# A decoder block's modulation rows: products moved into the mLSTM's chunk loop, four accumulators, other engines for some transfers

## The chip, the cores and the metric

The kernel runs on one core of one Trainium2 chip. The metric is the device time of one execution in microseconds (us). A core has TensorE (PE, with its weight loads shown apart as PEld), VectorE (DVE), ScalarE (ACT), GpSimd (POOL) and SyncE (SP). Any of SP, ACT and POOL can issue a transfer; each engine takes its instructions strictly in the order in which they stand in its program, and a transfer that must wait holds up what stands behind it on the engine that issues it.

## The reference

One decoder layer over 1024 tokens of width 1024. Six rows of 1024 numbers, the modulation, are a product of one vector with a 1024 x 6144 matrix; the rows gate1, shift2, scale2 and gate2 (numbers 2 to 5) are the ones that the change is about. One of the four mixers is an mLSTM that carries a state from one chunk of 128 tokens to the next.

```python
cond = jax.nn.silu(c)
mod = cond @ w_ada[layer] + b_ada[layer]
shift1, scale1, gate1, shift2, scale2, gate2 = jnp.split(mod[:, None, :], 6, axis=-1)
h = rms_norm(x, w_norm1) * (1.0 + scale1) + shift1
x = x + gate1 * hybrid_mixer(h, w_in, w_out, ...)
h = rms_norm(x, w_norm2) * (1.0 + scale2) + shift2
x = x + gate2 * hierarchical_moe(h, ...)
...
def mlstm_chunkwise(q, k, v, i_pre, f_pre):   # one chunk of 128 tokens at a time
    ...
    C_new = scale * C + einsum('blhd,blhe->bhde', vc * w_s, kc)
    w = einsum('bcthd,bcshd->bctsh', q, k) * exp(log_d - m_t)
    num = einsum('bctsh,bcshd->bcthd', w, v) + inter * einsum('bchde,bcthe->bcthd', C_in, q)
```

## The kernel before

A first stage (about 0 to 80 us) norms the input, makes the rows shift1 and scale1, and leaves the normed input transposed in SBUF as a high and a low half, `hH` and `hL`. Then come the projections with `w_in`, block of 256 columns by block: `load_w` brings a block in two halves of 512 KB (four of the eight row tiles each) into the buffer `wraw`, of which there is one; ACT copies a half to its high part `wh`, and DVE subtracts to get the low part `wl` (function `split`, L53 and L61). Each projection is three products per row tile, (wh, hH), (wl, hH) and (wh, hL), in one PSUM tile of the pool `ps` (two buffers) that ACT evicts. The mLSTM's four blocks are LQ and LK (products of 128x512), then LV and LO (128x256, eight groups of 24 each); the sigmoid of LO's groups, `so`, goes to DRAM (`so_d`) and is read back later as `ym`.

Beside these, `modulation` makes the four rows. For each row, DVE accumulates eight tiles of `w_ada` times a column of `cond` into the tile `macc` (L552 the first, L554 the others); the tiles `mw`, 512 KB each in three buffers, are loaded by SP (L550). Then TensorE sums over the partitions with two products of a column of ones and a half of `macc` (written `pq<-macc,ones`), DVE adds the bias row (L562, for the third row L564 too), and ACT stores the row to `mod_d`. There is one `macc`.

Behind the projections of the mLSTM stands its loop over eight chunks t. A chunk takes a broadcast row block `rb` (SP), the products `pq<-qT,kT`, the exponentials `ex` on DVE and ACT, DVE's products of `ex` with those scores (L612), the products `pq<-va,ex`, and from the second chunk on `pq<-C,qT` with the state; a transpose of `kT`, products `pq<-vw,kt` and four DVE steps (L647) make the next state. Between the chunks' products TensorE takes the projections of the next block group, MX0 to MX2 (`ssd_inputs`): their `wraw`, `wh` and `wl` are made in the meantime, their groups are evicted by ACT as `craw` and `xbc`, and three DVE steps (L680) and a SiLU make the convolution.

A scheduler sets the order of the instructions on each engine over this whole stretch: it interleaves the projections, the modulation, the chunk loop and the MX blocks by its own estimates, so that code that stands behind in the text can stand ahead in an engine's program. What an engine's program holds is fixed once the kernel is built.

## Time and profile before

| | before |
|---|---|
| median of 3 runs | 1274.83 us (1273.33 to 1276.05) |
| profiled execution, its own time | 1273.05 us |
| its span | 1271.3 us |
| TensorE busy in it | 1153.3 us (91%) |
| DVE / ACT / POOL busy | 801.5 / 589.3 / 326.3 us |
| mean granted TensorE clock | 0.966 of full speed |

The span is what the trace covers, and the execution's own time is 1.75 us more. Times in the rows further down count from the span's start. A row of a timeline gives the start, the duration, the engine with the line of the code, the operation, what it writes and reads, how many instructions the row holds, and in brackets the idle time before it with what ended that idle time.

### The profile page before, as it was taken

The page shows a single profiled execution, that of the slowest core. Times are in us where ns is not written, and L with a number is a line of the kernel's source. Part 1 is how long each engine was busy: PE and PEld are TensorE (multiplying, and loading weights), DVE is VectorE, ACT ScalarE, POOL GpSimd, SP SyncE. Part 2 cuts the span into 40 slices and gives each one's busy share as a digit, 9 for nine tenths or more (in the row PEclk, how much of TensorE's full clock was granted, in tenths as well). Part 3 has the DMA queues.
Part 4 walks back from the last instruction along what each step waited for, and adds up shares of the span by engine and source line. Part 5 has one row for each costly group of instructions (what it writes and reads, how often), then busy time and mean ns, then how long its engine had stood idle before and what let it go on. Part 6 is the DMA issues. An engine that isn't in the chain of part 4 may idle for free. (4 is left out here: it accounts for less than half of the span.)

```text
span 1271.3 us, 18583 instructions
## 1 busy us (share of the span) xinstructions
PE 1153.3 (91%) x6455; PEld 868.1 (68%) x6455; DVE 801.5 (63%) x1460; ACT 589.3 (46%) x909; POOL 326.3 (26%) x314
## 2 busy tenths in 40 slices
PE   4689879999999899999959999999999999999981
PEld 3577667879998788787747754466676557665660
DVE  6976667757643488488878941335654564555674
ACT  6442114354743488344437841224553443554563
POOL 2420000002102277333321942102322132222111
PEclk8699999999999999999969999999999999999996
DMA  9614884222221123675477999999999998999975
GB/s 268 203 32 149 261 271 118 89 71 53 73 60 34 42 65 111 203 267 199 162 296 290 328 332 377 376 403 372 385 378 378 357 389 317 341 367 384 337 274 198
DMA packets 96452, 305.48 MB, mean 240 GB/s; under 512 B 15106, under 2 KB 53756, under 8 KB 71772
## 3 DMA queue, kind: packets, MB, share of 16 engines
q1 hardware_dynamic: 84762, 284.47, 60.9%
q0 software_dynamic: 8464, 17.13, 5.8%
q10 hardware_dynamic: 3122, 2.56, 0.6%
q8 instruction: 57, 0.93, 0.3%
q14 instruction: 47, 0.39, 0.1%
HBM read 283.86 MB, written 32.06 MB: 249 GB/s over the span
## 5 line engine op out<-in xcount | busy, mean ns | idle before, releaser
L1649 POOL DMA_INDIRECT x_d<-yt,tabi x34 | 62.1, 1827 | 240.7 <-DVE yt L1623 186.7
L56 PE MATMUL ps<-wu,xTs 128*64 128x512 f32 x256 | 119.5, 599 | 1.8 <-DMA wu<-in_w_expert_up_dram 1.8
L56 PE MATMUL ps<-wg,xTs 128*64 128x512 f32 x256 | 119.8, 599 | 0.0
L56 PE MATMUL ps<-wh,hH 128*128 128x256 f32 (+1 forms) x336 | 96.9, 289 | 8.2 <-ACT so L53 4.9
L56 PE MATMUL ps<-wl,hH 128*128 128x256 f32 (+1 forms) x336 | 95.8, 286 | 0.0
L56 PE MATMUL ps<-wh,hL 128*128 128x256 f32 (+1 forms) x336 | 95.2, 288 | 0.0
L56 PE MATMUL ps<-hH,wh 128*128 128x512 f32 x224 | 89.1, 398 | 0.5 <-ACT xbc L53 0.4
L56 PE MATMUL ps<-hH,wl 128*128 128x512 f32 x224 | 89.4, 399 | 0.0
L56 PE MATMUL ps<-hL,wh 128*128 128x512 f32 x224 | 89.0, 397 | 0.0
L56 PEld LDWEIGHTS ps<-wh,hH 128*128 128x128 f32 x336 | 64.4, 192 | 11.4 <-ACT so L53 5.5
L56 PE MATMUL ps<-split,xTH 128*128 128x512 f32 x200 | 69.4, 403 | 1.0
L56 PEld LDWEIGHTS ps<-wg,xTs 128*64 128x64 f32 x256 | 32.1, 136 | 54.6 <-issue 51.3
L1640 POOL TENSOR_TENSOR yt<-yt,g2bc 128x1024 f32<-128x1024 f32 x14 | 33.7, 2409 | 137.5 <-ACT yt L53 121.4
L53 ACT ACT_TABLE_LOAD x47 | 60.3, 1283 | 17.7 <-DVE xbc L680 5.9
L53 ACT ACTIVATE xTH<-pq 128x512 fp32r<-128x512 f32 x33 | 18.4, 592 | 100.9 <-PE pq L1664 100.9
L56 PE MATMUL ps<-wh,xTH 128*128 128x512 f32 (+1 forms) x156 | 63.8, 409 | 1.4 <-PEq L1869 0.5
L56 PEld LDWEIGHTS ps<-wl,hH 128*128 128x128 f32 x336 | 64.1, 191 | 0.9 <-issue 0.9
L61 DVE TENSOR_TENSOR wl<-wu,wh 128x1024 fp32r<-128x1024 f32 x39 | 47.2, 1222 | 27.4 <-ACT wh L53 26.7
L56 PEld LDWEIGHTS ps<-wh,hL 128*128 128x128 f32 x336 | 64.3, 194 | 0.0
L56 PE MATMUL ps<-wl,xTH 128*128 128x512 f32 (+1 forms) x156 | 61.3, 393 | 0.5 <-DVE wl L61 0.5
L56 PE MATMUL pq<-wd,aTs 128*64 128x512 f32 x256 | 58.7, 597 | 3.0 <-PEq L1857 2.1
L53 ACT ACTIVATE sg<-ps 128x512 f32<-128x512 f32 (+1 forms) x32 | 18.9, 592 | 91.1 <-PE ps L56 49.8
(550 smaller groups left out, 3241.2 us busy)
## 6 DMA issues: line engine op xcount, KB each, us to landing
wg<-in_w_expert_gate_dram SPq DMA_DIRECT2D x64, 1024.0 KB, 9.5
wu<-in_w_expert_up_dram SPq DMA_DIRECT2D x64, 1024.0 KB, 8.1
wd<-in_w_expert_down_dram SPq DMA_DIRECT2D x64, 1024.0 KB, 7.5
mw<-in_w_ada_dram SPq DMA_DIRECT2D x32, 512.0 KB, 5.0
wraw<-in_w_in_dram SPq DMA_DIRECT2D x20, 512.0 KB, 3.6
xt<-in_x_dram SPq DMA_DIRECT2D x16, 512.0 KB, 4.1
wt<-in_w_ada_dram SPq DMA_DIRECT2D x16, 512.0 KB, 5.4
woraw<-in_w_out_dram SPq DMA_DIRECT2D x16, 256.0 KB, 3.4
```

Of the source, the lines that this page charges most:

```text
L53: return nc.scalar.activation(o, i, f, **kw)
L56: return nc.tensor.matmul(o, l, r, start=start, stop=stop)
L61: (eng or nc.vector).tensor_sub(lo, src, hi.bitcast(F32))
L1640: nc.gpsimd.tensor_mul(yt[:, on_dve * 512:], yt[:, on_dve * 512:], g2bc[:, on_dve * 512:])
L1649: nc.gpsimd.indirect_dma_start(out=x1_d, out_offset=bass.IndirectOffsetOnAxis(ap=tok, axis=0), in_=yt, in_offset=None, bounds_check=S - 1, ...
```

## The change

`modulation` keeps four accumulators (`macc0` to `macc3`) and runs all 32 loads and accumulations on end. The eight products with ones, the additions of the bias rows and the stores move into a function `mod_rows` that the chunk loop calls ahead of its third chunk (t == 2). The bias rows now take buffers of the tag `mw` (as 1x1024 of a 128x1024 tile) and are loaded by SP; the rows are stored by POOL. `load_w` takes the engine that loads: LK, LV and LO are loaded by ACT, the other blocks still by SP. The stores of `so` go from SP to ACT. Behind the change the lines of the code stand lower by 10 (L612 is L622, L680 is L690).

```diff
@@ -123,7 +123,7 @@
     hH = hpool.tile([P, KT, S], F32R, name="hH")
     hL = hpool.tile([P, KT, S], F32R, name="hL")
 
-    def load_w(*ranges):
+    def load_w(*ranges, first=nc.sync):
         n = sum(b - a for a, b in ranges)
         wh = wp.tile([P, KT, 272], F32R, name="wh")
         wl = wp.tile([P, KT, 272], F32R, name="wl")
@@ -131,7 +131,7 @@
             raw = wp.tile([P, 4, 272], F32, name="wraw", bufs=1)
             o = 0
             for i, (a, b) in enumerate(ranges):
-                (nc.sync if i % 2 == 0 else nc.scalar).dma_start(
+                (first if i % 2 == 0 else nc.scalar).dma_start(
                     raw[:, :, o:o + b - a],
                     w_in[k0 * P:(k0 + 4) * P, a:b].rearrange("(k p) g -> p k g", p=P))
                 o += b - a
@@ -542,9 +542,10 @@
     tab_d = dram.tile([S * NE, 4], F32, name="tab_d")
 
     def modulation(mp):
-        for i in range(4):
+
+        accs = [mp.tile([P, D], F32, name=f"macc{i}", bufs=1) for i in range(4)]
+        for i, acc in enumerate(accs):
             cs = slice((2 + i) * D, (3 + i) * D)
-            acc = mp.tile([P, D], F32, name="macc", bufs=1)
             for k in range(KT):
                 wt = mp.tile([P, D], F32, name="mw", bufs=3)
                 nc.sync.dma_start(wt, w_ada[k * P:(k + 1) * P, cs])
@@ -552,20 +553,27 @@
                     nc.vector.tensor_scalar(acc, wt, cond[:, k:k + 1], None, op0=OP.mult)
                 else:
                     nc.vector.scalar_tensor_tensor(acc, wt, cond[:, k:k + 1], acc, op0=OP.mult, op1=OP.add)
-            mr = mp.tile([1, 2, D], F32, name="mr", bufs=1)
-            nc.scalar.dma_start(mr[:, 0, :], b_ada[:, cs])
-            if i == 2:
-                nc.scalar.dma_start(mr[:, 1, :], w_norm2)
-            for c in (slice(0, 512), slice(512, D)):
-                o = pq1()
-                mm(o[0:1], ones[:, 0:1], acc[:, c], True, True)
-                nc.vector.tensor_add(mr[:, 0, c], mr[:, 0, c], o[0:1])
-            if i == 2:
-                nc.vector.scalar_tensor_tensor(mr[:, 0], mr[:, 0], 1.0, mr[:, 1], op0=OP.add, op1=OP.mult)
-            nc.scalar.dma_start(mod_d[i:i + 1], mr[:, 0])
-
-
-    def mlstm(ml, wk):
+
+        def mod_rows():
+            for i in range(4):
+                cs = slice((2 + i) * D, (3 + i) * D)
+                mr = mp.tile([P, D], F32, name="mr", tag="mw", bufs=3)[0:1]
+                nc.sync.dma_start(mr, b_ada[:, cs])
+                if i == 2:
+                    wr2 = mp.tile([P, D], F32, name="wr2", tag="mw", bufs=3)[0:1]
+                    nc.sync.dma_start(wr2, w_norm2)
+                for c in (slice(0, 512), slice(512, D)):
+                    o = pq1()
+                    mm(o[0:1], ones[:, 0:1], accs[i][:, c], True, True)
+                    nc.vector.tensor_add(mr[:, c], mr[:, c], o[0:1])
+                if i == 2:
+                    nc.vector.scalar_tensor_tensor(mr, mr, 1.0, wr2, op0=OP.add, op1=OP.mult)
+                nc.gpsimd.dma_start(mod_d[i:i + 1], mr)
+
+        return mod_rows
+
+
+    def mlstm(ml, wk, mod_rows):
         qT = ml.tile([P, 2, S], F32, name="qT")
         kT = ml.tile([P, 2, S], F32, name="kT")
         va = ml.tile([P, NT, NH, VW], F32, name="va")
@@ -575,26 +583,28 @@
         for j in range(2):
             for th in range(2):
                 act(qT[:, j, th * 512:(th + 1) * 512], chan_major(w, j, th), AF.Copy)
-        w = load_w((LK, LK + GW))
+        w = load_w((LK, LK + GW), first=nc.scalar)
         for j in range(2):
             for th in range(2):
                 act(kT[:, j, th * 512:(th + 1) * 512], chan_major(w, j, th), AF.Copy, scale=0.125)
-        w = load_w((LV, LV + GW))
+        w = load_w((LV, LV + GW), first=nc.scalar)
         for t in range(NT):
             act(va[:, t, :, :DH], heads(tok_major(w, t)[:, :GW], GW), AF.Copy)
         num = ml.tile([P, NT, NH, VW], F32, name="num")
         so_d = dram.tile([S, GW], F32, name="so_d")
-        w = load_w((LO, LO + GW))
+        w = load_w((LO, LO + GW), first=nc.scalar)
         for t in range(NT):
             so = wk.tile([P, GW], F32, name="so", tag="ym")
             act(so, tok_major(w, t)[:, :GW], AF.Sigmoid)
-            nc.sync.dma_start(so_d[t * P:(t + 1) * P], so)
+            nc.scalar.dma_start(so_d[t * P:(t + 1) * P], so)
 
         C = [ml.tile([P, 2, 2 * VW], F32, name=f"C{i}") for i in range(2)]
         for i in range(2):
             nc.gpsimd.memset(C[i], 0.0)
         for t in range(NT):
             ts = slice(t * P, (t + 1) * P)
+            if t == 2:
+                mod_rows()
             rb = wk.tile([P, NH, P], F32, name="rb")
             nc.sync.dma_start(rb, bc_rows_2d(nrow_d[:, t, :]))
 
@@ -943,8 +953,7 @@
     ml = pool(m1, "ml", "right")
     mlw = pool(m1, "mlw", "right", 2)
     m2 = ExitStack()
-    modulation(pool(m2, "mp", "right"))
-    mlstm(ml, mlw)
+    mlstm(ml, mlw, modulation(pool(m2, "mp", "right")))
     m2.close()
     m3 = ExitStack()
     xbc = ssd_inputs(pool(m3, "sA", "left"))
```

How the engines' programs change is read from their orders. **SP ahead of the block MX0, before.** The rows run from the last accumulator's loads to the first read-back of `so`; `wraw` is the first half of MX0.

```order
L550 DMA mw<-in_w_ada_dram 128x1024 x3
L591 DMA so_d<-so 128x256
L550 DMA mw<-in_w_ada_dram 128x1024 x2
L591 DMA so_d<-so 128x256 x2
L134 DMA wraw<-in_w_in_dram 128x4x256
L591 DMA so_d<-so 128x256 x3
L658 DMA ym<-so_d 128x2x256
```

MX0's first half is issued between stores of `so`, whose waits it shares.

**SP at the same place, now.** These are the last 16 loads of `mw` and what follows them.

```order
L551 DMA mw<-in_w_ada_dram 128x1024 x16
L561 DMA mr<-in_b_ada_dram 1x1024 x3
L609 DMA rb<-nrow_d 128x4x128
L134 DMA wraw<-in_w_in_dram 128x4x256
L668 DMA ym<-so_d 128x2x256
```

The first half of MX0 stood between stores of `so`, with the chunk loop's `rb` of the fourth chunk already issued; now it stands behind all of `mw`, three bias rows and that `rb`. The third of the three `mr` takes a buffer of `mw` and must wait until the last accumulation has read it. LO's loads and the stores of `so` are gone from SP.

**DVE at the start of the chunk loop, before.** `ex<-ex,pq` are the products of the first chunk, `wl` is the low part of MX0's first half.

```order
L554 SCALAR_TENSOR_TENSOR macc<-mw,cond,macc 128x1024 x5
L562 TENSOR_TENSOR mr<-mr,pq_982 1x512
L562 TENSOR_TENSOR mr<-mr,pq_985 1x512
L671 MEMSET craw 128x3
L673 MEMSET xbc_2085 128x3 x2
L673 MEMSET xbc_2218 128x3 x2
L673 MEMSET xbc_2351 128x3 x2
L612 TENSOR_TENSOR ex<-ex,pq_1688 128x2x128
L612 TENSOR_TENSOR ex<-ex,pq_1689 128x2x128
L61 TENSOR_TENSOR wl<-wraw,wh 128x4x256
```

So the first chunk's two products came right behind the additions of the last row, and only then the low part.

**DVE at the same place, now.** `macc_854` is the fourth accumulator, `L617` makes the second chunk's `ex`.

```order
L555 SCALAR_TENSOR_TENSOR macc_854<-mw,cond,macc_854 128x1024 x7
L61 TENSOR_TENSOR wl<-wraw,wh 128x4x256
L622 TENSOR_TENSOR ex<-ex,pq_1650 128x2x128
L622 TENSOR_TENSOR ex<-ex,pq_1651 128x2x128
L617 SCALAR_TENSOR_TENSOR ex<-rb,u,mpos 128x128 x4
L622 TENSOR_TENSOR ex<-ex,pq_1689 128x2x128
L657 SCALAR_TENSOR_TENSOR C_1645<-C_1644,csp,pq_1672 64x65 x4
L622 TENSOR_TENSOR ex<-ex,pq_1690 128x2x128
L627 TENSOR_TENSOR num<-pq_1703,escol 128x260
```

The low part of MX0's first half stood behind the first chunk's two products and now stands ahead of them, directly behind the last accumulation; the additions of the bias row are gone from here.

**TensorE at the last of the four rows, before.** `ps_1627` is a group of LO.

```order
L56 MATMUL ps_1627<-wh,hL 128x256
L56 MATMUL ps_1627<-wh,hH 128x256
L56 MATMUL pq_982<-macc,ones 1x512
L56 MATMUL pq_985<-macc,ones 1x512
L56 MATMUL ps_1627<-wl,hH 128x256
```

The pair of products with ones stood in the middle of a group of LO.

**TensorE ahead of the third chunk, now.** `pq_1715` belongs to the second chunk's state, the last row to the third chunk's scores.

```order
L645 MATMUL pq_1715<-ident,kT 128x128 x2
L56 MATMUL pq_1732<-macc_851,ones 1x512
L56 MATMUL pq_1715<-vw,kt 64x65 x4
L56 MATMUL pq_1735<-macc_851,ones 1x512
L56 MATMUL pq_1741<-macc_852,ones 1x512
L56 MATMUL pq_1744<-macc_852,ones 1x512
L56 MATMUL pq_1752<-macc_853,ones 1x512
L56 MATMUL pq_1755<-macc_853,ones 1x512
L56 MATMUL pq_1762<-macc_854,ones 1x512
L56 MATMUL pq_1765<-macc_854,ones 1x512
L56 MATMUL pq_1771<-qT,kT 128x128
```

The products with ones came in pairs, each pair between products of a projection, ahead of the chunk loop; seven of the eight now stand on end between two chunks, with no projection between them.

**DVE behind the chunk loop, before.** `hnv`, `num` and `ym` belong to the mLSTM's norms, L680 is the first step of MX0's convolution.

```order
L653 TENSOR_TENSOR d_2056<-num 128x8
L519 SCALAR_TENSOR_TENSOR hnv<-hnv,d_2041 128x8
L654 SCALAR_TENSOR_TENSOR d_2056<-d_2056,escol 128x8
L528 RECIPROCAL hnv<-hnv 128x8 x2
L529 TENSOR_TENSOR num<-num,hnv 128x8x64 x2
L659 TENSOR_TENSOR ym<-ym,num 128x512 x2
L517 TENSOR_REDUCE hnv<-hnq 128x8
L680 SCALAR_TENSOR_TENSOR xbc_2085<-craw,cols,xbc_2085 128x1024
```

The convolution's first step followed on the norms' steps, with no `wl` among them.

**DVE at the same place, now.** The rows begin with the first half of MX1.

```order
L61 TENSOR_TENSOR wl<-wraw,wh 128x4x256
L683 MEMSET xbc_2219 128x3 x2
L683 MEMSET xbc_2352 128x3 x2
L528 RECIPROCAL hnv<-hnv 128x8 x2
L529 TENSOR_TENSOR num<-num,hnv 128x8x64 x2
L669 TENSOR_TENSOR ym<-ym,num 128x512 x2
L517 TENSOR_REDUCE hnv<-hnq 128x8
L690 SCALAR_TENSOR_TENSOR xbc_2086<-craw,cols,xbc_2086 128x1024
```

The two `wl` of the block MX1, which stood inside the chunk loop, now stand here: the first ahead of this piece, the second two rows behind it, ahead of the second step of the convolution.

## Rows read from the trace of the kernel before

**Rows 1.** The page, busy time: busy us (share of the span) xinstructions.

```profile
PE 1153.3 (91%) x6455; PEld 868.1 (68%) x6455; DVE 801.5 (63%) x1460; ACT 589.3 (46%) x909; POOL 326.3 (26%) x314
```

**Rows 2.** Windows: stretch, length, busy us per engine, granted clock, DMA share, GB/s.

```profile
120.00:140.00 20.00, 17.61 (x78) 12.30 (x77) 12.24 (x12) 2.86 (x4) 0.00 (x0) 0.91 0.81 262
140.00:160.00 20.00, 18.41 (x145) 16.65 (x144) 14.99 (x18) 3.51 (x7) 2.44 (x2) 1.00 0.88 274
160.00:180.00 20.00, 16.39 (x125) 14.43 (x125) 13.93 (x16) 4.57 (x8) 0.00 (x0) 1.00 0.78 264
180.00:200.00 20.00, 15.14 (x110) 12.71 (x111) 9.14 (x15) 2.82 (x6) 0.00 (x0) 1.00 0.56 189
200.00:220.00 20.00, 20.00 (x157) 15.86 (x158) 18.35 (x58) 12.43 (x21) 2.50 (x4) 1.00 0.47 127
```

**Rows 3.** Waits, 112 to 200 us: total us, times, longest us.

```profile
DVE macc L554 <- DMA mw<-in_w_ada_dram: 12.8, 13, 1.6
...
PE ps L56 <- ACT so L53: 4.9, 3, 3.0
PE pq L56 <- DVE macc L554: 4.5, 2, 2.9
```

**Rows 4.** Timeline of SP, 110 to 200 us: issues of loads.

```profile
112.06 20.15 SPq L550 DMA_DIRECT2D mw<-in_w_ada_dram  x11
...
172.26 1.14 SPq L599 DMA_DIRECT2D rb<-nrow_d  x1
173.46 0.64 SPq L134 DMA_DIRECT2D wraw<-in_w_in_dram  x1
```

**Rows 5.** Timeline of DVE, 108 to 215 us.

```profile
116.62 1.23 DVE L61 TENSOR_TENSOR wl<-wraw,wh 128x1024 fp32r<-128x1024 f32 x1 [4.37 <-ACT wh L53]
...
118.60 2.60 DVE L554 SCALAR_TENSOR_TENSOR macc<-mw,cond,macc 128x1024 f32<-128x1024 f32 x2
...
130.57 1.28 DVE L554 SCALAR_TENSOR_TENSOR macc<-mw,cond,macc 128x1024 f32<-128x1024 f32 x1 [1.25 <-DMA mw<-in_w_ada_dram]
133.55 0.68 DVE L562 TENSOR_TENSOR mr<-mr,pq 1x512 f32<-1x512 f32 x1 [1.70 <-PE pq L56]
...
191.20 1.28 DVE L554 SCALAR_TENSOR_TENSOR macc<-mw,cond,macc 128x1024 f32<-128x1024 f32 x1 [1.25 <-DMA mw<-in_w_ada_dram]
...
201.40 1.23 DVE L61 TENSOR_TENSOR wl<-wraw,wh 128x1024 fp32r<-128x1024 f32 x1
```

**Rows 6.** Timeline of ACT, 172 to 202 us.

```profile
181.15 1.06 ACT L53 ACTIVATE wh<-wraw 128x1024 fp32r<-128x1024 f32 x1 [5.47 <-DMA wraw<-in_w_in_dram]
```

**Rows 7.** Issues of transfers, whole run: count, KB each, median us to landing.

```profile
mw<-in_w_ada_dram SPq DMA_DIRECT2D x32, 512.0 KB, 5.0
wraw<-in_w_in_dram SPq DMA_DIRECT2D x20, 512.0 KB, 3.6
...
rb<-nrow_d SPq DMA_DIRECT2D x8, 256.0 KB, 6.3
```

**Rows 8.** Timeline of TensorE, 128 to 202 us.

```profile
131.96 3.27 PE L56 MATMUL pq<-macc,ones 128*1 128x512 f32 x4 [2.39 <-issue]
...
192.66 1.88 PE L56 MATMUL pq<-macc,ones 128*1 128x512 f32 x4
...
201.10 1.16 PE L56 MATMUL pq<-va,ex 128*128 128x130 f32 x8
```

**Rows 9.** Timeline of TensorE and window, 70 to 76 us.

```profile
71.58 1.09 PE L289 MATMUL pq<-ident,acc 128*128 128x128 f32 x4 [4.46 <-DVE acc L211]
...
72.00:74.00 2.00, 2.00 (x11) 2.00 (x10) 1.33 (x8) 0.17 (x1) 0.27 (x1) 0.50 0.00 0
```

**Rows 10.** Timelines of ACT and TensorE behind the chunk loop.

```profile
242.84 1.28 ACT L53 ACT_TABLE_LOAD   x1 [2.40 <-DVE xbc L680]
...
246.41 0.51 PE L56 MATMUL ps<-hH,wh 128*128 128x512 f32 x1 [0.39 <-ACT xbc L53]
```

**Rows 11.** Stores of POOL: issue to landing.

```profile
nrow_d<-nrow POOLq DMA_DIRECT2D x1, 16.0 KB, 1.7
```

## The prediction

> **What bounds the kernel now.** I read the page first. TensorE is busy for 91% of the span [rows 1], so the change can gain where TensorE waits, and lose where it gives TensorE something to wait for. The windows of 20 us over the stretch that the change touches show where that is [rows 2]: TensorE is busy for 17.61, 18.41, 16.39 and 15.14 of 20 us from 120 to 200, and for all 20 of them from 200 to 220, when the chunk loop runs between MX projections. So 12.45 us are idle from 120 to 200, and none in the loop. The list of waits [rows 3] says what ended these idle times. The accumulations wait 12.8 us for their tiles, 13 times, TensorE 4.5 us for the accumulations (the products with ones stand in its program ahead of projections that are ready), and 4.9 us for evictions of LO, which hang on stores of `so` that SP issues late among the loads. Transfers fill 0.78 to 0.88 of the DMA engines' time from 120 to 180 [rows 2]: the stretch is bound by the modulation's 16 MB, and TensorE waits wherever the two are tied together.
>
> **What is untied.** With the products gone from between the projections, and LO's loads and the `so` stores off SP, nothing holds the projections of LK, LV and LO but their own weights. The last product before the chunk loop's `va,ex` would be ready 12.45 us of waits and four pairs of products earlier. A pair is 1.88 us [rows 8], a row of four records, so one product takes 0.94; the first pair took 3.27. That is 12.45 + 3.27 + 3 x 1.88 = 21.4 us, so TensorE would stand at the chunk loop at about 201.1 - 21.4 = 180 in place of 201.1 [rows 8].
>
> **What it is tied to instead.** On DVE the first chunk's products `ex<-ex,pq` now stand behind the last accumulation and behind `wl` of MX0's first half, and on SP that half is issued behind the third bias row, which waits for the last accumulation's buffer. So the loop begins at the end of the accumulations plus a chain, however early TensorE is there.
>
> The end of the accumulations: the second tile can start when the `wl` ahead of it ends, 116.62 + 1.23 = 117.9 [rows 5]. While only `mw` was being loaded (eleven in a row on SP [rows 4]), tiles 2 to 8 came from 118.60 to 130.57, six steps of 2.0 us each [rows 5], and one accumulation is 1.28 us. With 30 steps of 2.0 the last ends at 117.9 + 60 + 1.3 = 179.2. That is the low bound, since in that stretch no other transfer ran. Over the whole of before, 118.60 to 191.20, a step was 2.42 us, with all the loads between and DVE's waits for `macc`; at that rate the end is 191.8, the high bound. LO's two halves and three `rb` come into the stream, 2 x 512 and 3 x 256 KB [rows 7], 3.5 tiles' worth: 7 us if bytes decide, nothing if the three buffers' turnaround does. I take half, 3.5, which gives 182.7.
>
> The chain behind it: three bias rows, an `rb` and then `wraw` are issued; an `rb` and a `wraw` behind it were issued 1.2 us apart, 172.26 and 173.46 [rows 4], and I take 1.2 for the whole, since the first two bias rows wait for nothing so late. The half lands 3.6 us after its issue as the run's median [rows 7], and took from 173.46 to 181.15, 7.7 us, behind an `rb` with `mw` beside it [rows 4, 6]. Here it has the `rb` ahead of it but no more `mw`: I take the middle, 5.6. ACT's `wh` is 1.06 [rows 6], DVE's `wl` 1.23 [rows 5], and a first `ex` product 0.4 (an estimate: a quarter of an accumulation's columns, 0.32, rounded up). Together 9.5 us, and `va,ex` of the first chunk at 182.7 + 9.5 = 192.2, which is **8.9 us earlier** than 201.10.
>
> **What the chunk loop takes on.** The loop had no idle TensorE time [rows 2], so its added work counts in full: eight products with ones of 0.94 are **7.5 us**. DVE's additions, 0.68 each [rows 5], are shorter than a product and lie beside it; DVE was busy for 18.35 of 20 us [rows 2], and in 7.5 us more of TensorE it has room for their 5.4. The first products come after some 12 us without work. How that starts is seen at 71.58: after 4.46 us of waiting the granted clock was 0.50 for the next 2 us, the lower of the two levels, 1.2 GHz [rows 9]. Two us at half speed lose **1.0 us**.
>
> A rule of the Trainium skill speaks against the change. It says in "DMA: Bandwidth & Descriptors", section "Issuing engines are not separate DMA queues", that transfers issued by different engines run on the same 16 DMA engines and interleave, so that another issuer saves only the sequencer's time. No row here compares two issuers; by the rule the accumulations would keep the old rate, which is the first slow rival below.
>
> **What stands behind the loop.** The two `wl` of MX1, of which the first took 1.23 us in the loop [rows 5], move from inside the loop, where they lay beside projections, to behind it, between the norms and the convolution of MX0. The chain convolution, SiLU, eviction is what TensorE waits for already: ACT's table load stands 2.40 us for DVE's last convolution step and TensorE then 0.39 us for ACT's eviction [rows 10]. So nothing covers them, and the wait grows by their sum, 2 x 1.23 = **2.5 us**. The bound below is 0: if MX0's groups end later than the convolution can start, they are hidden.
>
> The stores of `mod_d` by POOL and the bias rows by SP have no reader on the way: a POOL store landed in 1.7 us [rows 11], and the last bias row's load has a chunk of the loop to land (eight chunks lie between 201.10 and 242.84 [rows 8, 10], so at most 5.2 us each). I put them at nothing; what covers them is the loop's other work, and the price without it is among the rivals.
>
> **The sum.** -8.9 + 7.5 + 1.0 + 2.5 = +2.1 us. The profiled execution took 1273.05 us, 1.8 under the median of the runs shown, so 1275.2 for such an execution and **1276.9** on the median. The stretch's idle time moves: from small waits inside the projections to one wait ahead of the loop, and the products' cover is given up. What a measurement of this kernel can tell from no change is 0.2%, 2.55 us: the forecast is within it.
>
> **The rivals.** *Faster: a clean stream.* LO's loads by ACT fit into the buffers' turnaround, the accumulations end at 179.2 and MX0's half lands in 3.6 us. Then the first `va,ex` is at 179.2 + 7.5 = 186.7, 14.4 us earlier, and the sum is -3.4: 1271.4. For it speaks that a step waits for its three buffers, each 5.0 us to land [rows 7] and 1.28 to be read, 6.3 / 3 = 2.1, near the measured 2.0; against it the DMA share of 0.8 and more, which leaves little. If the `wl` behind the loop are hidden too, 1268.9. Chance 0.25, with the lone case that only the 2.5 falls away (1274.4, still within 0.2%) another 0.08.
>
> *Slower: the stream keeps its rate.* All transfers share the DMA engines, and 2.42 us a step is what bytes allow beside them. The accumulations end at 191.8, the loop starts at 201.3, and nothing is gained: 0.2 + 7.5 + 1.0 + 2.5 = +11.2, **1286.0**. The point from which it decides is an end at 183.2, a step of 2.13 us: every later end is slower by more than 0.2%. Against it speaks that 4.5 us of before's waits are tied to the single `macc` [rows 3], which no longer exists. Chance 0.13.
>
> *Slower: the rows' chain.* The last bias row is loaded behind two `rb`, the norm's row and a `wraw` on SP, and its buffer is free only when an earlier row has been stored. DVE's additions wait for it, and the chunk loop's steps stand behind them on DVE. An `rb` took 6.3 us to land [rows 7] and a store 1.7 [rows 11]: 8.0 us, of which a chunk covers at most 5.2. Between 2.8 and 8.0 I take the middle, 5.4: 1282.3. Chance 0.12.
>
> **How the numbers follow.** My forecast has 0.42: its own range is 1274 to 1279.5, of which 0.30 lies within 0.2% and 0.12 above. Faster 0.25; same 0.30 + 0.08 = 0.38; slower 0.12 + 0.13 + 0.12 = 0.37. The range goes from 1269, just above the clean stream's best, to 1284, short of the full old rate.
>
> **What would show it.** In the changed trace: DVE's last accumulation ends near 183 (179 by the clean stream, 191 by the old rate); TensorE has one wait of about 10 us ended by ACT's `wh` or DVE's `ex` ahead of the first `va,ex`, which starts near 192; a stretch at half clock follows; seven products with ones in a row take about 0.94 us each with no wait between; and behind the loop the wait for MX0's convolution is near 2.8 us. The forecast is wrong if TensorE still waits inside LK, LV or LO, if the `wl` of MX1 hold nothing, or if the products with ones wait for bias rows.

## The result: slower by 0.87%, and the profile after

The changed kernel took 1286.06 us in the median of 4 runs (1283.74 to 1287.60), before 1274.73: a ratio of 1.0087, 95% interval 1.0066 to 1.0109. The prediction was 1276.9 within 1269 to 1284, with "same" only just the likeliest (0.38, against 0.37 for slower); it was wrong. The two profiled executions, which the rest compares, took 1284.83 and 1273.05 us, 11.8 apart.

Two windows of 20 us of the changed kernel, in the columns of [rows 2]:

```profile
160.00:180.00 20.00, 19.65 (x166) 19.45 (x165) 12.24 (x10) 3.59 (x7) 0.00 (x0) 1.00 0.86 274
180.00:200.00 20.00, 9.41 (x64) 8.33 (x64) 7.02 (x7) 2.37 (x5) 0.00 (x0) 0.77 0.52 166
```

TensorE's waits are gone from 160 to 180 us, 19.65 us busy in place of 16.39, and have come together from 180 to 200, where it is busy for 9.41 us in place of 15.14. The timeline of DVE shows when the accumulations end and what stands behind them:

```profile
118.14 1.22 DVE L61 TENSOR_TENSOR wl<-wraw,wh 128x1024 fp32r<-128x1024 f32 x1
...
119.41 2.61 DVE L555 SCALAR_TENSOR_TENSOR macc<-mw,cond,macc 128x1024 f32<-128x1024 f32 x2
...
126.22 0.88 DVE L617 SCALAR_TENSOR_TENSOR ex<-rb,u,mpos 128x128 f32<-128x128 f32 x3 [2.57 <-DMA rb<-nrow_d]
...
147.69 0.88 DVE L617 SCALAR_TENSOR_TENSOR ex<-rb,u,mpos 128x128 f32<-128x128 f32 x3 [2.52 <-DMA rb<-nrow_d]
...
149.51 1.23 DVE L61 TENSOR_TENSOR wl<-wraw,wh 128x1024 fp32r<-128x1024 f32 x1 [0.95 <-ACT wh L53]
...
155.91 0.75 DVE L553 TENSOR_SCALAR macc<-mw,cond 128x1024 f32<-128x1024 f32 x1 [1.20 <-DMA mw<-in_w_ada_dram]
...
186.53 1.28 DVE L555 SCALAR_TENSOR_TENSOR macc<-mw,cond,macc 128x1024 f32<-128x1024 f32 x1 [0.41 <-DMA mw<-in_w_ada_dram]
...
196.31 1.23 DVE L61 TENSOR_TENSOR wl<-wraw,wh 128x1024 fp32r<-128x1024 f32 x1 [8.50 <-ACT wh L53]
```

The first row is the `wl` ahead of the second tile, the second the tile itself, the last but one the last accumulation: it ends at 187.8, and 30 steps from 119.41 to 186.53 are 2.24 us each. Between stand rows of `ex` and a `wl` for which DVE waited 2.57, 2.52 and 0.95 us. Behind the second and third of these waits tiles of `mw` lay ready (three accumulations followed that waited for none); behind the first DVE had to wait 1.10 us more for a tile. The step was not the same all along: the fifteen steps up to the row at 155.91 (the first tile of the third row) took 2.43 us each, the fifteen from there on, with none of these rows among them, 2.04. The timeline of SP, where the third of the bias rows waits for the last accumulation:

```profile
183.59 4.48 SPq L561 DMA_DIRECT2D mr<-in_b_ada_dram  x3
188.12 0.39 SPq L609 DMA_DIRECT2D rb<-nrow_d  x1
188.56 0.50 SPq L134 DMA_DIRECT2D wraw<-in_w_in_dram  x1
```

The first half of MX0 is issued at 188.56. In the kernel before, both its halves lay inside the stream, issued at 152.52 and 173.46; the `wraw` between the stores of `so` and the `wl` behind the first chunk's products, which the orders ahead call MX0's, are MX1's. Rows of SP, ACT and DVE of the kernel before show it:

```profile
152.52 0.46 SPq L134 DMA_DIRECT2D wraw<-in_w_in_dram  x1
...
167.47 0.39 ACT L53 ACTIVATE so<-ps 128x256 f32<-128x256 f32 x1 [0.20 <-PE ps L56]
...
168.96 1.22 DVE L61 TENSOR_TENSOR wl<-wraw,wh 128x1024 fp32r<-128x1024 f32 x1
```

LO's first group, which needs both of LO's `wl`, was evicted at 167.47, and the blocks come in order: the `wl` at 168.96 and the next, at 182.24, are MX0's, the one at 201.40 [rows 5] is MX1's first. So the change moved MX0's halves from inside the stream to behind it. ACT's timeline, now (the second row is MX0's `wh`, the first is spoken of below):

```profile
140.87 0.66 ACT L53 ACTIVATE va<-ps 128x256 f32<-128x256 f32 x2 [7.80 <-DVE wl L61]
...
195.23 1.06 ACT L53 ACTIVATE wh<-wraw 128x1024 fp32r<-128x1024 f32 x1 [11.05 <-DMA wraw<-in_w_in_dram]
```

It had landed at 195.23, 6.7 us after its issue. DVE's `wl` ends at 197.5 (the last row of DVE above), and TensorE's timeline goes on from there:

```profile
141.30 0.58 PE L56 MATMUL ps<-wh,hH 128*128 128x256 f32 x1 [4.17 <-ACT va L53]
...
196.34 0.79 PE L56 MATMUL ps<-hH,wh 128*128 128x512 f32 x1 [9.52 <-ACT wh L53]
...
198.19 1.07 PE L56 MATMUL pq<-va,ex 128*128 128x130 f32 x4
...
204.88 1.02 PE L56 MATMUL pq<-macc,ones 128*1 128x512 f32 x2
...
206.22 1.02 PE L56 MATMUL pq<-macc,ones 128*1 128x512 f32 x2
...
238.28 0.94 PE L56 MATMUL pq<-va,ex 128*128 128x130 f32 x7
...
254.55 0.50 PE L56 MATMUL ps<-hH,wh 128*128 128x512 f32 x1 [2.93 <-ACT xbc L53]
```

TensorE stands idle for 9.52 us, multiplies the first chunk's `va,ex` at 198.19 and the last chunk's at 238.28; the eight products with ones lie between, two records for each: 1.02 us for the first and 6.17 us for the other seven. Behind the loop it waits 2.93 us for the convolution in place of 0.39. The last chunk's row of the kernel before, on the same timeline, is:

```profile
233.15 1.06 PE L56 MATMUL pq<-va,ex 128*128 128x130 f32 x8
```

So the loop, from the first to the last chunk's `va,ex`, took 233.15 - 201.10 = 32.05 us before [rows 8] and takes 40.09 now. The first MX1 group comes at 254.55 in place of 246.41 [rows 10].

Up to that group TensorE takes the same products in both kernels, only in another order, so the 8.1 us can also be read from windows that begin at 112 us, where both kernels begin to load `mw`, and end at the group (before, then now):

```profile
112.00:246.41 134.41, 121.58 (x805) 99.82 (x805) 94.66 (x185) 37.99 (x66) 5.56 (x7) 0.99 0.61 196
112.00:254.55 142.55, 123.98 (x808) 104.14 (x806) 94.03 (x186) 38.58 (x66) 7.49 (x11) 0.94 0.58 187
```

TensorE is idle for 18.6 us in place of 12.8, which is 5.7 of the 8.1; the other 2.4 are longer busy time, with a mean granted clock of 0.94 in place of 0.99.

### The profile page after: what moved, and what is told of

The parts are those of the page before. It is cut to its first block, busy times and chain, and to the rows that moved or that the text cites. A ratio compares the mean times of both kernels' runs of the same rounds, so it can differ in the third digit from the quotient of the medians.

```text
span 1282.9 us, 18585 instructions
## 1 busy us (share of the span) xinstructions
PE 1159.5 (90%) x6455; PEld 876.0 (68%) x6455; DVE 800.2 (62%) x1460; ACT 589.6 (46%) x909; POOL 328.6 (26%) x318
## 5 line engine op out<-in xcount | busy, mean ns | idle before, releaser
L56 PEld LDWEIGHTS ps<-wg,xTs 128*64 128x64 f32 x256 | 32.1, 136 | 58.3 <-issue 52.8
L56 PE MATMUL ps<-wh,xTL 128*128 128x512 f32 (+1 forms) x156 | 61.0, 391 | 0.1
```

The lines of the kernel that those rows point to most:

```text
L56: return nc.tensor.matmul(o, l, r, start=start, stop=stop)
```

## The experiments

All were read at the same four places: the end of the last accumulation, the first chunk's `va,ex`, the last chunk's, and the first product of MX1 (the 97th of 128x512 behind LO's groups). All times are us of the profiled execution, from the timelines; the median is that of all runs, and the ratio goes against the kernel before on the same chip. The column "MX" counts MX0's products inside the loop: they come 0.23 us apart, and a loop that holds fewer of them is shorter for that reason alone.

| kernel | last acc. ends | first `va,ex` | loop | MX | last `va,ex` to MX1 | median | ratio, 95% |
|---|---|---|---|---|---|---|---|
| before | 192.5 | 201.1 | 32.1 | 43 | 13.3 | 1274.7 | |
| changed | 187.8 | 198.2 | 40.1 | 41 | 16.3 | 1286.1 | 1.0066 to 1.0109 |
| e1 moves to ACT only | 192.5 | 201.9 | 32.0 | 43 | 13.3 | 1274.8 | 0.9987 to 1.0006 |
| e2 no moves to ACT | 181.6 | 188.9 | 58.9 | | | 1289.8 | 1.0091 to 1.0137 |
| e3 products ahead of the loop | 190.9 | 207.7 | 35.9 | 53 | 12.8 | 1287.1 | 1.0066 to 1.0113 |
| e7 no products | 190.4 | 202.7 | 32.6 | 37 | 16.5 | | |
| e10 bias rows by POOL | 191.6 | 203.2 | 39.6 | 45 | 13.2 | 1282.6 | 1.0034 to 1.0073 |
| e6 `rb` by POOL | 194.8 | 199.8 | 40.0 | 42 | 14.7 | 1278.3 | 1.0004 to 1.0040 |
| c1 ACT, 4 buffers | 181.1 | 199.0 | 32.1 | 43 | 13.3 | 1271.1 | 0.9947 to 0.9985 |
| c3 POOL, 4 buffers | 185.7 | 202.9 | 32.3 | 43 | 13.3 | 1277.2 | 0.9982 to 1.0029 |
| e12 products back | 200.8 | 206.5 | 29.5 | 29 | 16.8 | 1283.4 | 1.0057 to 1.0094 |
| c2 2 accumulators, 5 buffers | 180.4 | 199.7 | 32.1 | 43 | 13.3 | 1271.2 | 0.9955 to 0.9983 |
| c4 the same, rows later | 169.8 | 189.4 | 30.5 | 22 | 19.2 | 1271.8 | 0.9960 to 0.9986 |
| c5 3 accumulators, 4 buffers | 176.6 | 195.5 | 32.4 | 43 | 14.8 | 1269.8 | 0.9957 to 0.9985 |
| e14 half tiles, 6 buffers | 175.6 | 189.0 | 37.4 | 35 | 16.8 | 1272.5 | 0.9972 to 1.0001 |
| e15 the same, products ahead | 178.1 | 200.5 | 32.1 | 42 | 13.8 | 1272.1 | 0.9958 to 0.9986 |

**One part alone: the moves to ACT (e1), and all but them (e2).** e1 is the kernel before with

```diff
-    def load_w(*ranges):
+    def load_w(*ranges, first=nc.sync):
-        w = load_w((LK, LK + GW))
+        w = load_w((LK, LK + GW), first=nc.scalar)      # LV, LO alike
-            nc.sync.dma_start(so_d[t * P:(t + 1) * P], so)
+            nc.scalar.dma_start(so_d[t * P:(t + 1) * P], so)
```

and e2 the changed kernel with these three lines as they were.

> The kernel before with only the moves to ACT (loads of LK, LV and LO, stores of so); the modulation keeps its one accumulator and its products stay between the projections. Theory A (the loss comes from the eight products with ones in the chunk loop, 8 us, from the block MX0 that is split late, and from 3 us behind the loop; the moves to ACT do no harm): the products keep their cover, so the time is that of before or a little less, 1270 to 1276. Rival B (the moves to ACT cost the time, since ACT stands at a load for its buffer with evictions behind it): 1280 or more.

> The changed kernel with the loads of LK, LV and LO and the stores of so back on SP. In SP's order all 32 loads of mw now stand ahead of the second half of LV and of both halves of LO. Theory A: these wait for the last accumulations, TensorE stands idle from about 140 to 185 us, and the time is 1310 or more, so the moves to ACT are what makes the uninterrupted stream bearable. Rival B (ACT's waits are the loss): the time falls to 1275 to 1280.

e1 took the time of before, so the moves to ACT neither gain nor cost by themselves (its last accumulation ends at 192.5, as before). e2 went as theory A said in kind, not in size: 1290, not 1310. SP's timeline and TensorE's:

```profile
112.22 62.65 SPq L551 DMA_DIRECT2D mw<-in_w_ada_dram  x32
174.93 0.43 SPq L134 DMA_DIRECT2D wraw<-in_w_in_dram  x1
```

```profile
182.90 0.80 PE L56 MATMUL ps<-wh,hH 128*128 128x256 f32 x2 [28.19 <-ACT wh L53]
```

The first half of LO (LV's eight groups had been evicted by 154.5, so it is not LV's) is issued behind all 32 tiles, at 174.93, and TensorE waits 28.19 us for it. It lost less than I said because the chunk loop had been let into the projections that were still missing: its first `va,ex` came at 188.9. The accumulations of e2 (DVE) serve as a measure: until 174.93 nothing else is loaded beside the 32 tiles, and no other row stands between them on DVE.

```profile
118.97 2.61 DVE L555 SCALAR_TENSOR_TENSOR macc<-mw,cond,macc 128x1024 f32<-128x1024 f32 x2 [0.29 <-DMA mw<-in_w_ada_dram]
...
180.36 1.28 DVE L555 SCALAR_TENSOR_TENSOR macc<-mw,cond,macc 128x1024 f32<-128x1024 f32 x1 [2.49 <-DMA mw<-in_w_ada_dram]
```

Thirty steps take 61.4 us, 2.05 each.

**Where the products with ones stand (e3), and what they cost (e7).**

```diff
-            if t == 2:
+            if t == 0:
                 mod_rows()
```

> The changed kernel with the eight products with ones ahead of the first chunk instead of the third, where TensorE now waits 9.5 us. Theory A: six of them fall into that wait and two follow the last accumulation, so the loop loses its 8 us again: 1278 to 1280. Rival C (the loss lies in the rearranged later stages): no change against the changed kernel, 1284 to 1288.

```diff
-                    o = pq1()
-                    mm(o[0:1], ones[:, 0:1], accs[i][:, c], True, True)
-                    nc.vector.tensor_add(mr[:, c], mr[:, c], o[0:1])
+                    nc.vector.tensor_add(mr[:, c], mr[:, c], accs[i][0:1, c])
```

> The changed kernel without the eight products with ones: the bias row is added to the first row of each accumulator, so the sum over the 128 partitions is left out. Theory A: 7.5 us of TensorE's time leave the loop, 1277 to 1280. Rival C: 1284 to 1288.

In e7 the loop takes 32.6 us (the first and last chunk's rows of TensorE; the last row's chunk goes on for six more records):

```profile
202.65 0.64 PE L56 MATMUL pq<-va,ex 128*128 128x130 f32 x2
...
235.23 0.39 PE L56 MATMUL pq<-va,ex 128*128 128x130 f32 x2
```

The loop is 40.1 - 32.6 = 7.5 us shorter, but it also holds four MX products fewer, 0.9 us; the products' own rows in the changed kernel add up to 1.02 + 6.17 = 7.2 us, 0.90 each. So they cost the loop about 7 us. What they cost the kernel no run shows: e7's whole time, 1398.81 us, is not compared: its expert stage, working on other values, took longer, and its stream ended 2.6 us later than the changed kernel's. e3 took the products out of the loop (35.9 us, with 53 MX products in it in place of 41) and gained nothing. Its DVE and TensorE show why:

```profile
199.44 1.23 DVE L61 TENSOR_TENSOR wl<-wraw,wh 128x1024 fp32r<-128x1024 f32 x1 [8.49 <-ACT wh L53]
200.58 1.86 DVE L568 TENSOR_TENSOR mr<-mr,pq 1x512 f32<-1x512 f32 x3
```

```profile
201.30 3.57 PE L56 MATMUL pq<-macc,ones 128*1 128x512 f32 x4 [5.62 <-DVE mr L568]
...
207.71 0.49 PE L56 MATMUL pq<-va,ex 128*128 128x130 f32 x2 [0.60 <-DVE ex L622]
```

DVE's additions stood behind MX0's `wl`, which waits for its load; the products before them held the PSUM buffers (the row of TensorE's wait names an addition as what ended it, after 5.62 us), and the first `va,ex` came at 207.71, 9.5 us later. Six of the eight did fall into the wait, as theory A said, but its expectation was wrong: the wait for MX0's half moved with them.

**SP freed of the waits (e10, e6).** e10: `nc.gpsimd.dma_start(mr, ...)` and `wr2` alike in place of `nc.sync`. e6: `nc.gpsimd.dma_start(rb, ...)`.

> The changed kernel with the bias rows and the second norm's row loaded by POOL, so that on SP the first half of MX0 follows the last loads of mw without waiting for the last accumulation. Theory A (the loop starts late because MX0's half is issued only behind the last accumulation: 188.6 us, landed 195.2): the half is issued near 184 and lands by 191, the first product of va and ex comes near 193 in place of 198.2, and the time is 1280 to 1283. Rival (the accumulations themselves set the start): no gain, 1285 to 1288.

> The changed kernel with the loop's row blocks rb loaded by POOL instead of SP. By the program's order MX0's two halves then stand inside the loads of mw, and the low part behind the first chunk's products on DVE, as before the change. Theory A: the first product of va and ex follows the last accumulation by about 2 us, near 192 (the bytes of MX0's halves now lie ahead of it); the products with ones still cost 8 us in the loop: 1280 to 1283. Rival: DVE's waits for rb (5 us) were what slowed the accumulations, then they end near 183 and the time is 1275 to 1278.

e10's median fell to 1282.6, but its profiled execution (1287.87, the longest of its ten) shows another start than expected: the program's order now puts both halves of MX0 ahead of the first chunk on DVE.

```profile
194.82 1.23 DVE L61 TENSOR_TENSOR wl<-wraw,wh 128x1024 fp32r<-128x1024 f32 x1 [3.23 <-ACT wh L53]
201.57 1.23 DVE L61 TENSOR_TENSOR wl<-wraw,wh 128x1024 fp32r<-128x1024 f32 x1 [5.52 <-ACT wh L53]
202.71 0.41 DVE L622 TENSOR_TENSOR ex<-ex,pq 128x256 f32<-128x256 f32 x1
```

It tells one thing clearly: here no `wl` of MX1 stands among the convolution's steps, and the stretch behind the loop is 13.2 us again in place of 16.3. From the last chunk's `va,ex` to the convolution's third step on DVE it is 8.5 us, as before (8.3), against 11.4 in the changed kernel. In e6 the expected 192 became 199.8, since the accumulations ended at 194.8. DVE:

```profile
122.92 1.28 DVE L555 SCALAR_TENSOR_TENSOR macc<-mw,cond,macc 128x1024 f32<-128x1024 f32 x1
...
192.22 2.61 DVE L555 SCALAR_TENSOR_TENSOR macc<-mw,cond,macc 128x1024 f32<-128x1024 f32 x2 [2.94 <-DMA mw<-in_w_ada_dram]
```

So its rival failed as well: DVE now waited for an `rb` only ahead of the first accumulation (6.88 us at 120.27) and no more between them, and yet thirty steps, from 122.92 to 193.54, took 70.6 us against the changed kernel's 67.1. Five halves of weights and two `rb` were loaded beside them, against two halves and three `rb`. The time was 8 us below the changed kernel, but the first product of MX1 comes at 254.5 in both and the loop holds about as many MX products: the gain arose behind this stretch, and what made it was not looked into.

**The stream's rate (c1, c3).** Both are e1 with `bufs=4` for `mw`; in c3 `first=nc.gpsimd`.

> The kernel before with the moves to ACT and four buffers of mw instead of three; products with ones between the projections, one accumulator. Theory T (a step of the accumulations is the three buffers' turnaround, 5.1 us to land and 1.3 to be read): the step falls to about 1.6 us, the loads end near 172, TensorE no longer waits for accumulations, 1266 to 1271. Theory B (the stretch is bound by bytes at about 268 GB/s, whatever the order): the stretch's GB/s stays at 265 to 275, the last accumulation ends at 186 to 190, 1272 to 1276.

> As the kernel with the moves to ACT and four buffers of mw, but with LK, LV and LO loaded by POOL, so that no eviction on ACT stands behind a load that waits for its buffer. Theory T: 1265 to 1270. Theory B: 1270 to 1275; in both less than with the loads on ACT by the 4 us that TensorE waited at 141 us in the changed kernel for an eviction behind such a load, as far as they lie on the path.

Theory T held for the stream's rate, with a step of 2.01 us in place of e1's 2.42 (not the 1.6 that I gave), and the time came out at the upper edge of its range. From 113 to 150 us before moved 282 GB/s (the last column; e1 moved 283), c1 319:

```profile
113.00:150.00 37.00, 34.61 (x191) 27.84 (x189) 23.38 (x20) 7.01 (x11) 2.44 (x2) 0.95 0.85 282
```

```profile
113.00:150.00 37.00, 31.58 (x168) 25.07 (x168) 25.03 (x24) 6.50 (x10) 2.41 (x2) 0.98 0.89 319
```

The accumulations end 11.4 us earlier than in e1 (181.1, not the 172 that I gave), but the loop starts 3 us earlier: it hangs on TensorE's own work, as before, and three waits for accumulations, 8.5 us together, still stand ahead of it. c3 did not do better, but worse than c1 by 6 us, outside both theories; why was not looked into.

**The products back between the projections (e12).** `mod_rows()` and its call are gone; the body stands inside the loop over the accumulators:

```diff
         for i, acc in enumerate(accs):
             ...
+            mr = mp.tile([P, D], F32, name="mr", tag="mw", bufs=3)[0:1]
+            nc.sync.dma_start(mr, b_ada[:, cs])
+            ...
+            nc.gpsimd.dma_start(mod_d[i:i + 1], mr)
```

> The changed kernel with one thing undone: each row's two products, additions and store follow its accumulations again, between the projections; four accumulators, the bias rows in mw's buffers, the stores by POOL and the moves to ACT stay. Theory A: the loop from the first to the last product of va and ex takes 32 us again in place of 40.1, and the low parts of MX1 lie in it: 1272 to 1277. Rival (the four accumulators, the shared buffers or the other engines for the transfers cost the time): 1282 to 1287.

This was theory A's plainest test, and it missed: 1283.4. The loop did fall, to 29.5 us (2.8 of it because it holds twelve MX products fewer), but the stream ended at 200.8. SP's and DVE's timelines:

```profile
129.73 0.25 SPq L557 DMA_DIRECT2D mr<-in_b_ada_dram  x1
```

```profile
185.88 1.28 DVE L555 SCALAR_TENSOR_TENSOR macc<-mw,cond,macc 128x1024 f32<-128x1024 f32 x1 [4.56 <-DMA mw<-in_w_ada_dram]
...
199.53 1.28 DVE L555 SCALAR_TENSOR_TENSOR macc<-mw,cond,macc 128x1024 f32<-128x1024 f32 x1 [1.34 <-DMA mw<-in_w_ada_dram]
```

A bias row takes one of three buffers of `mw` from its load (129.73) until the row is stored, and the stream goes on with two; at 185.88 DVE waited 4.56 us for a tile. What the loop won, the start lost.

**Versions with more buffers (c2, c4, c5).** All have the moves to ACT and the bias row in a buffer of `mw`. c2: `macc` with 2 buffers, `mw` with 5. c4: c2 with `row(i)` written behind `accumulate(i + 1)`. c5: 3 and 4 buffers, and `row(i)` behind `accumulate(i + 2)`:

```diff
+        for i in range(4):
+            accumulate(i)
+            if i >= 2:
+                row(i - 2)
+        return lambda: [row(i) for i in range(2, 4)]      # called at LO's seventh group
```

> The kernel before with the moves to ACT, two accumulators and five buffers of mw (the bias row in one of them). If a step of the accumulations is the buffers' turnaround, the last accumulation ends near 174 (181 with four buffers, 192 with three) and TensorE's waits for accumulations shrink: 1266 to 1271. If bytes bind from four buffers on, 1270 to 1273 as with four.

> As the kernel with two accumulators and five buffers, with each row's products written behind the next row's accumulations and the last row's ahead of LO's seventh group. By the program's order the first three pairs stand where they stood, and the last pair is parted around LO's groups. Turnaround theory: 1265 to 1270; if the products' places decide, no better than the kernel it is made from.

> Moves to ACT, three accumulators, four buffers of mw, each row's products written two rows later, so that the products of the last two rows stand behind LO's sixth group, where their accumulations have ended. Theory: TensorE waits for accumulations at one place at most (the second row), and what it wins there shows in the start of the loop: 1264 to 1270. Rival (the loop starts when MX0's half is split, whatever TensorE waited before): 1270 to 1275.

c2 comes out as c1 does; since a bias row takes one of its five buffers, this doesn't tell what a fifth buffer of loads alone would bring. c4, whose 32 loads stand unbroken on SP, moved most, its loop started at 189.4 and its first product of MX1 came at 239.1, 7.3 us earlier than before; yet its time is that of c2. At the experts' first product it was 4.0 us ahead (731.5 against 735.5), and its expert products took 2.3 us longer (457.4 against 455.1), so the gain was given back behind this stretch; why is open. c5 has the lowest median, 1269.75 us against 1274.48, but by their ratios c1, c2, c4 and c5 can't be told apart: all four are faster than both kernels, by about 0.3% than the one before. The window of 113 to 150 us of c4, and that of e2, whose 32 loads stand as unbroken on SP, in three buffers:

```profile
113.00:150.00 37.00, 35.96 (x208) 29.13 (x207) 30.05 (x26) 7.24 (x12) 2.39 (x2) 1.00 0.97 354
```

```profile
113.00:150.00 37.00, 37.00 (x240) 33.56 (x239) 21.19 (x18) 5.78 (x11) 1.68 (x2) 1.00 0.83 270
```

In c4 the DMA engines are busy for 0.97 of it and move 354 GB/s, so that little more is to be had by buffers.

**The stream alone, within the change (e14), and the products ahead of the loop with it (e15).**

```diff
-                wt = mp.tile([P, D], F32, name="mw", bufs=3)
-                nc.sync.dma_start(wt, w_ada[k * P:(k + 1) * P, cs])
+                for c in (slice(0, 512), slice(512, D)):
+                    wt = mp.tile([P, 512], F32, name="mw", bufs=6)
+                    nc.sync.dma_start(wt, w_ada[k * P:(k + 1) * P, (2 + i) * D + c.start:(2 + i) * D + c.stop])
```

> The changed kernel with the tiles mw halved to 128x512, six buffers in the same room, twice as many accumulations of half the length; the bias rows in halves too. By the program's order the row blocks rb and MX0's halves are all issued behind the loads of mw, and on DVE the first chunk's products follow the last accumulation with no low part between. Start theory (the loop starts late because the stream of mw in three buffers ends late and a chain of MX0's half follows it): the last accumulation ends at 172 to 180, the first product of va and ex comes at 183 to 190 in place of 198.2, the loop still takes 40 us, and the time is 1271 to 1279. Rival (the start is not what the time hangs on): 1283 to 1288.

> As the kernel with halved tiles, with the eight products with ones ahead of the first chunk. Theory: the loop takes 32 to 34 us; the low part of MX0 and the additions stand ahead of the first chunk on DVE again, so part of the gain goes into the start: first product of va and ex near 192, 1269 to 1277. Rival (additions behind the low part hold PSUM buffers and TensorE, as with whole tiles): the loop starts 8 us later than with the products in the loop, and the two times are alike.

DVE and TensorE of e14:

```profile
174.86 0.75 DVE L556 SCALAR_TENSOR_TENSOR macc<-mw,cond,macc 128x512 f32<-128x512 f32 x1 [0.53 <-DMA mw<-in_w_ada_dram]
...
186.18 0.75 DVE L623 TENSOR_TENSOR ex<-ex,pq 128x256 f32<-128x256 f32 x2 [7.36 <-PE pq L56]
```

```profile
188.95 1.05 PE L56 MATMUL pq<-va,ex 128*128 128x130 f32 x8
...
226.38 0.39 PE L56 MATMUL pq<-va,ex 128*128 128x130 f32 x2
...
243.13 0.50 PE L56 MATMUL ps<-hH,wh 128*128 128x512 f32 x1 [1.34 <-ACT xbc L53]
```

The last accumulation ends at 175.6, the first `va,ex` comes 9.2 us earlier than in the changed kernel, the loop keeps most of the products' price (37.4 us), and the median falls by 13.6 us. So the change's whole loss can be had back without taking the products out of the loop. That the stream's end alone did it isn't shown: e14 also puts the first chunk's products on DVE ahead of MX0's low part, and TensorE's last long wait ahead of the loop (5.89 us at 180.18) now ends with an eviction of LO, not with the stream. In e15 the loop is back at 32.1, and the start went from 189.0 to 200.5, as its rival said; the two times are alike.

## Why the prediction was wrong, step by step

**The first term failed: the start of the loop, -8.9 us, was -2.9.** The prediction built it as 117.9 + 60 + 3.5 + 1.3 + 9.5 = 192.2; the rows give 119.4 + 60 + 7.1 + 1.3 + 10.4 = 198.2. Of the 6.0 us, 0.9 lie in the chain behind the accumulations (MX0's half landed in 6.7 us, not 5.6), 1.5 in a second tile that started later, since the `wl` ahead of it on DVE now stood behind the first tile and its wait, and 3.6 in what LO's two halves and three `rb` cost the stream. I had seen that they cost 7 us if bytes decide and nothing if the three buffers' turnaround does, and had taken half, without a row that favoured half: 1.0 us for each tile's worth. The clean step of 2.0 was right (e2, 2.05; the changed kernel's second fifteen steps, 2.04).

What was moved beside the stream cost more than that in each of these runs with three buffers: thirty steps took 61.4 us in e2, with nothing beside them for most of it; 67.1 in the changed kernel and 69.8 and 69.3 in e3 and e7, with 3.5 tiles' worth of halves and `rb`; 70.6 in e6, with 6; 72.6 before, with 7. Against e2 that is 1.5 to 2.4 us for each. Whether the shared transfers themselves or DVE's rows for them made the difference isn't shown apart. DVE did wait 6.0 us for two `rb` and a `wh` in the changed kernel with accumulations queued behind, but 19.3 us for tiles; and e6, with 3.7 us of such waits, had the longer stream. No fixed ceiling on bytes held the rate down: unbroken loads moved 270 GB/s with three buffers (e2) and 354 with five (c4).

**Second term, the loop: +8.5 forecast, +8.0 measured.** The products' rows take 7.2, not 7.5, and the loop holds two MX products fewer (0.5), so that about 1.3 are left. The first chunk ran at the lower level of the clock (1.2 GHz), for which the sum had 1.0; from 198 to 200 us the granted clock (the third number from the end) was 0.50, in the next 2 us 0.73:

```profile
198.00:200.00 2.00, 2.00 (x10) 2.00 (x10) 0.20 (x1) 0.28 (x1) 0.00 (x0) 0.50 0.57 139
```

**Third term, behind the loop: +2.5 forecast, +3.0 measured.** The wait grew by 2.5 (2.93 against 0.39), the rest is two more MX products. It is smaller in e10 (1.30), where no `wl` stands among the convolution's steps. In e14 both stand there, but eight more MX products lie behind the loop and the wait is 1.34: they hid a part, as the bound of 0 allowed.

**Not in the sum: +3.7.** -2.9 + 8.0 + 3.0 is 8.1, the distance at MX1's group; the executions differ by 11.8. The first product of the experts comes 9.6 us later (745.1 against 735.5), so 1.5 arose in the stages between, and the expert products took 1.7 longer (456.8 against 455.1). The prediction put all of this at nothing. Much of it may be spread of single executions: e1, whose later stages are those of before, lies 0.8 us behind at MX1's group and 3.1 at its end, and over the profiled runs here the expert products took from 454.9 to 457.6. What the 1.5 is was not tested.

**The rivals.** "The stream keeps its rate" gave 1286.0, the measured number, but not for its reason, and so by luck: the step fell from 2.42 to 2.24, the start did come 2.9 us earlier, and 3.7 us outside the sum made up for it. Its point of decision, an end at 183.2, held. The rows' chain did not show: the products with ones ran at 0.88 us on end (6.17 us for seven), with no wait for a bias row. The Trainium skill's rule ("DMA: Bandwidth & Descriptors", "Issuing engines are not separate DMA queues"), that another issuer saves only the sequencer's time, agrees with e1, where ACT issues what SP did: a ratio of 0.9997, and a step of 2.42 as before.

**TensorE's own waits were also misjudged, at no cost.** I expected none inside LK, LV and LO. There was one of 4.17 us at 141.30: on ACT the load of LO's half waits until DVE's `wl` frees `wraw`, and evictions stand behind it for 7.80 us (the first row of ACT above). As the loop waited for the stream anyway, it cost nothing here.

## What to carry to other kernels

Work that lies between other work has to be priced again at the place that it is moved to: eight products that lay between projections take 7.2 us of a loop in which TensorE was already busy, and moving them ahead of it (e3) gained nothing, back between the projections (e12) little. A stream through few buffers is slowed by what is moved beside it: here each tile's worth cost 1.5 us or more where I had taken 1.0, so count these transfers, and try another buffer (c1) or halved tiles (e14) before anything is rearranged around the stream. And follow what is issued behind the last buffer's wait: here half a weight block stood there, and with it the loop.

## What the runs showed of the hardware that was not expected

The rate of the loads rose with the number of tiles that could be on their way: with unbroken loads of 512 KB on SP it was 270 GB/s in three buffers (e2) and 354 in five (c4, where a bias row holds one of them at times), while the DMA engines' share rose from 0.83 to 0.97; with other loads between, 283 in three (e1) and 319 in four (c1).

Transfers issued by POOL took more of the DMA engines' time for the same bytes. From 222 to 231 us the changed kernel and e6 load the same two `rb`, 0.52 MB, and next to nothing else (packets, MB, share of 16 engines; by SP, then by POOL):

```profile
q1 hardware_dynamic: 1056, 0.52, 21.5%
```

```profile
q0 software_dynamic: 160, 0.52, 38.1%
```

They landed about as fast: 4.5 us by SP (the changed kernel, issued at 206.20), 4.9 to 5.0 by POOL in e6's loop. Beside the stream of `mw` both were slower, 7.7 us by SP (before, issued at 152.00) and 7.1 to 9.2 by POOL.
